# Modulation sums as four quarters, a convolution moved behind a third projection unit, and state-space set-up dealt out evenly, in a two-layer hybrid encoder

## The chip, the cores and the metric

The kernel runs on one core of one Trainium2 chip. What is measured is the device time of one execution in microseconds (us), as the median of several runs. The engines are named as the profile names them: PE is TensorE's matmul side and PEld its weight loads, DVE is VectorE, ACT is ScalarE, POOL is GpSimd, SP is SyncE, whose queue loads the weights. "PEclk" or "granted clock" is TensorE's clock as a share of full speed (1.00 is 2.4 GHz, 0.50 is 1.2 GHz).

## The reference

Two layers, each of them feed-forward, mixer, feed-forward, over 256 positions of width 1024 in float32:

```python
cond = silu(c)[:, None, :]
for l in range(2):
    mod = cond @ mod_w[l] + mod_b[l]               # nine vectors of 1024
    sh1, sc1, g1, sh2, sc2, g2, sh3, sc3, g3 = split(mod, 9)
    h = modulate(rms_norm(x, ffn1_norm[l]), sh1, sc1)
    x = x + 0.5 * g1 * swiglu_ffn(h, w_gu, w_down)      # 1024 -> 2 x 2816 -> 1024
    h = modulate(rms_norm(x, mix_norm[l]), sh2, sc2)
    x = x + g2 * hybrid_mixer(h, ...)    # attention | state space (S5) | convolution
    h = modulate(rms_norm(x, ffn2_norm[l]), sh3, sc3)
    x = x + 0.5 * g3 * swiglu_ffn(h, w_gu, w_down)
return rms_norm(x, final_norm)
```

The state-space part needs, before its layer's mixer, powers of a complex number per state (`PW`), their products with another one (`PQ`), and from these two large tables, W and O, that multiply B and C. The convolution is a depthwise one over 31 positions of 256 channels, after a gate.

## The kernel before

**Weights.** All weights are streamed once, in units of 128x1024, by SP's queue into six buffers `raw`. A matmul in float32 is made of three (`mm3`, L328 to L330): ACT makes the rounded part `hi` of a unit (L100), DVE the rest `lo` (L102, about 1.2 us), and PE takes hi·hi, lo·hi and hi·lo. `hi` and `lo` have six pairs of buffers, five in the mixer. So every unit of weights that PE uses has first passed ACT and then DVE, and PE takes the units in the order of the stream.

**The feed-forward part** goes over 11 blocks of 256 columns of the inner width. For a block, four units make gate and up products in PSUM (`ps_gt`, or `ps_gu` and `ps_gs` at the start), ACT makes silu, DVE the product `h` (L742; L756 at the start) and its `hTl` (L746), and two further units make the down products `ps_y`. The next block's `ps_gt` goes into the bank that `h` frees.

**Modulation.** mod_w of what comes later is streamed between the units of the feed-forward parts. DVE multiplies a half unit by its column of `cond` and adds it to an accumulator `macc` (L365, 128x512, two buffers; eight of them make one half of a vector). When both halves of a vector are there, `mod_flush` sums them over the partitions: a product with a matrix of ones on PE for each half (L389), a copy to `mrow` on ACT (L391), and POOL's DMAs of the row to DRAM and back as columns. Of the 16 flushes, six stand in the first feed-forward part of layer 0 (FFN1 of layer 0), three in its second (FFN2 of layer 0), six in FFN1 of layer 1 and one in FFN2 of layer 1.

**Set-up of the state space.** `ssm_small` and `ssm_layer` are generators that write out a few small instructions and then yield. They are stepped from the feed-forward code: layer 0's by `SSTART` steps for each of eight rounds at the start of the program and then by a hook at every tick of FFN1 of layer 0 (a tick is one unit; 41 ticks), layer 1's at the 45 ticks of FFN2 of layer 0. `SLOTS0` and `SLOTS1` are the first tick, the number of ticks, and the steps. The tables are made of products of 128x512 on DVE (L1011, L1013; sums in L1015), four for each of W and O and for each of two factors.

**The mixer** is written by several threads of code whose turns stand in a list of letters, `MIX_ORDER`: W issues the next unit's products of the input projection (A, C, four of B, four of Q), C is the convolution's thread (`conv_thread`), S the state space's, the others the attention. The convolution's input is written to `uT`, copied by DMAs on ACT's and POOL's queues to `U4` (`U` in the profile) in four shifted copies, and then multiplied in 64 products of 128x256 (L1404, `ps_cv`).

**Order.** The framework's scheduler fixes each engine's order ahead of the run, from the order of the code and modelled times; every engine then takes its list strictly in turn. So an instruction that waits holds up all that stand behind it on its engine.

Of the kernel before, what the change touches and what calls it, by code (L numbers as in the profile page):

```python
# [13 lines left out]
AF = mybir.ActivationFunctionType  # L14
# [12 lines left out]
ADG = (((0,),(1,),(2,3)),((0,1,2,3),))  # L27
HIP = 150
HIPT = 50
SLOTS0 = (4, 40, 2)  # L30
SSTART = 4
SLOTS1 = (2, 60, 2)
UW = 264
NEG_INADM = -3.0e38
NEG_TAKEN = -3.3e38
# [9 lines left out]

MIX_ORDER = """
W K S K K W K J I J J I W I S J S I W I J J I S W I J I J S W C C C I J J I S W
I J I J S I J C S W W C S W a b S N a C a C S S b b a C a b C b a a b b b C b b
b
"""  # L50

# [80 lines left out]
def kernel(  # L132
# [31 lines left out]
    def s2(shape, nm, tg="a", dtype=F32):  # L164
        return two_p.tile(shape, dtype, tag="s2" + tg, name=nm, bufs=S2B[tg])
# [217 lines left out]
    def mod_flush():  # L383
        while len(finished) >= 2:
            l, m, _, acc0 = finished.pop(0)
            acc1 = finished.pop(0)[3]
            ps = bank(ps_m, "ps_mod")
            for h, acc in enumerate((acc0, acc1)):
                nc.tensor.matmul(ps[32 * h:32 * h + 32, :], ones, acc, start=True, stop=True, tile_position=(0, 32 * h))  # L389
            r = s2([64, 512], "mrow")  # L390
            nc.scalar.activation(r, ps[0:64, :], AF.Copy, scale=0.5 if m in (2, 8) else 1.0)  # L391
            d = spill[(l, m)] = tc.dram_tile([1, D], F32, name=f"spill{l}_{m}")
            for h in range(2):
                nc.gpsimd.dma_start(d[:, 512 * h:512 * h + 512], r[32 * h:32 * h + 1, :])  # L394
            if m % 3 != 2:
                nc.gpsimd.dma_start(mc(l, m), d[0].rearrange("(k p) -> p k", p=P))
            if m % 3 == 1:
                nc.gpsimd.tensor_scalar_add(mc(l, m), mc(l, m), 1.0)
                n0 = 8 * (L * (m // 3) + l)
                nc.gpsimd.tensor_mul(mc(l, m), mc(l, m), ncol[:, n0:n0 + 8])  # L400
# [421 lines left out]
    def ssm_small(l):  # L822
# [7 lines left out]
        def B(nm, shape):  # L830
            n = math.prod(shape)
            if not pool8 or pool8[-1][1] + n > 2048:
                pool8.append([b8([P, 2048], "sp_tmp"), 0])
            t_, o_ = pool8[-1]
            pool8[-1][1] += n
            v_ = t_[:, o_:o_ + n]
            return v_ if len(shape) == 1 else v_.rearrange("p (d n) -> p d n", d=shape[0])
# [92 lines left out]
        yield  # L930

        PQr, PQi = B("pqr", [8, NL]), B("pqi", [8, NL])
        u8, v8 = B("u8", [8, NL]), B("v8", [8, NL])
        qrb = qr.rearrange("p (o n) -> p o n", o=1).to_broadcast([P, 8, NL])
        qib = qi.rearrange("p (o n) -> p o n", o=1).to_broadcast([P, 8, NL])
        cmul(PQr, PQi, PWr[:, 0:8, :], PWi[:, 0:8, :], qrb, qib, u8, v8)
        yield

        cA, cB = T("cA", [8, NL]), T("cB", [8, NL])
        lo_, hi_ = slice(0, 64), slice(64, 128)  # L940
        for tau in range(8):
            d_ = 7 - tau
            cp(cA[lo_, tau, :], PQr[lo_, d_, :])
            cp(cA[hi_, tau, :], PQi[hi_, d_, :])
            cp(cB[lo_, tau, :], PQi[lo_, d_, :], -1.0)
            cp(cB[hi_, tau, :], PQr[hi_, d_, :])
            if tau % 2:
                yield
        oA, oB = T("oA", [8, NL]), T("oB", [8, NL])
        cp(oA[lo_], PWr[lo_, 1:9, :])  # L950
        cp(oA[hi_], PWi[hi_, 1:9, :], -1.0)
# [140 lines left out]
    def mixer(l, finish):  # L1092
# [30 lines left out]
        def project():  # L1123

            def xT(k):
                return [v["f"][:, k].rearrange("p t n -> p (t n)") for v in (xTh, xTl)]

            for i in IN_ORDER:
                if i == "A":

                    us = [st.get() for _ in range(4)]
                    pin["A"] = [bank(ps_g, f"ps_in{t}")[:, :328] for t in range(2)]
                    pin["K"] = bank(ps_m, "ps_kT")
                    for t in range(2):
                        for k in range(8):
                            wh, wl = us[k // 2]
                            cs = slice(424 * (k % 2) + 96, 424 * (k % 2) + 424)
                            mm3(pin["A"][t], xTh[t][:, k, :], xTl[t][:, k, :], wh[:, cs], wl[:, cs], k == 0, k == 7)
                    for k in range(8):
                        wh, wl = us[k // 2]  # L1140
                        cs = slice(424 * (k % 2), 424 * (k % 2) + 96)
                        mm3(pin["K"][:96, :256], wh[:, cs], wl[:, cs], *xT(k), k == 0, k == 7)
                        if k % 2:
                            st.done()
                    yield
                elif i == "C":
                    us = [st.get() for _ in range(2)]
                    pin["C"] = bank(ps_g, "ps_inC")
                    for j in range(2):
                        for k in range(8):  # L1150
                            wh, wl = us[k // 4]
                            cs = slice(256 * (k % 4) + P * j, 256 * (k % 4) + P * j + P)
                            mm3(pin["C"][:, 256 * j:256 * j + 256], wh[:, cs], wl[:, cs], *xT(k), k == 0, k == 7)
                            if j and k % 4 == 3:
                                st.done()
                    yield
                else:
                    pin[i] = [bank(ps_g, f"ps_in{i}") for _ in range(2)]
                    for n_ in range(4):
                        wh, wl = st.get()  # L1160
                        o = slice(256 * (n_ // 2), 256 * (n_ // 2) + 256)
                        for k4 in range(4):
                            k = 4 * (n_ % 2) + k4
                            for j in range(2):
                                cs = slice(256 * k4 + P * j, 256 * k4 + P * j + P)
                                mm3(pin[i][j][:, o], wh[:, cs], wl[:, cs], *xT(k), k == 0, k == 7)
                        st.done()
                        yield

# [218 lines left out]
        def conv_thread():  # L1388
# [9 lines left out]
                yield  # L1398
            yield
            pc = abank(1, "ps_cv")  # L1400
            for ct in range(2):
                for b in range(8):
                    for q in range(4):
                        nc.tensor.matmul(pc[32 * q:32 * q + 32, 256 * ct:256 * ct + 256], SS["W4"][:, 32 * ct + 8 * q + b, :],  # L1404
                                         U4[:, q, ct, b:b + 256], start=(b == 0), stop=(b == 7),
                                         tile_position=(0, 32 * q))
# [83 lines left out]
        for g_ in gens:  # L1490
            yield from g_

    def stages(gen, first, n, per):

        def hook(u):
            if first <= u < first + n:
                for _ in range(per):
                    next(gen, None)
            elif u >= first + n:
                for _ in gen:  # L1500
                    pass
        return hook
# [74 lines left out]
```

## Time and profile before

| | |
|---|---|
| time, median of 3 runs | 1168.14 us (1165.55 to 1171.28) |
| time of the profiled execution | 1179.52 us |
| its span | 1177.7 us |
| mean granted clock of TensorE | 0.947 |
| PE, DVE, ACT, POOL busy | 1104.6, 880.2, 574.4, 78.3 us |

The profiled execution took 11.4 us more than the median of the runs. The feed-forward parts lie, in its time, at about 0 to 262 us (the first 70 us are the start: loads, norms and the first blocks), 425 to 620, 640 to 830, and 995 to the end; the mixers between them. An engine's busy time is the time in which at least one of its instructions was under way; instructions on DVE and PE overlap a little, so the distance between the starts of two neighbours is what one costs in a full queue.

### The profile page before, as it was taken

Reading aid. Unit: us, or ns where it says so; the run is one execution under the profiler, and the core shown is the slowest. Engines: PE = TensorE matmul, PEld = TensorE weight load, DVE = VectorE, ACT = ScalarE, POOL = GpSimd, SP = SyncE. Lnnn points to the kernel's source line nnn. Section 1 sums busy time; section 2 is a strip of 40 time slices with the busy share of each in tenths; the row PEclk is TensorE's granted clock in tenths of the full one; section 3 lists DMA queues with packets and bytes.
Section 4 is the critical chain, followed back from the end, with each engine's and each line's share of the span. In section 5 each row is a group of like instructions: output and inputs, shape, how many; then the busy total and the mean of one; then the engine's idle time right before and its main releaser. Section 6 shows DMA issues by size and latency. Waiting matters only on the chain.

```text
span 1177.7 us, 19146 instructions
## 1 busy us (share of the span) xinstructions
PE 1104.6 (94%) x6979; PEld 944.4 (80%) x6979; DVE 880.2 (75%) x1763; ACT 574.4 (49%) x1035; POOL 78.3 (7%) x144
## 2 busy tenths in 40 slices
PE   5959999998989999889998999999899998999996
PEld 3549888877876779788986888888698687999986
DVE  4779888887667888887757888887667677665655
ACT  4484434346427565744445444443553656544442
POOL 5000021000021000001000000100000000000000
PEclk9979989999798999989999999999989699999999
DMA  9957999995452268678773999989355224767651
GB/s 249 295 182 248 310 312 319 325 282 148 122 118 87 90 197 293 207 229 259 226 223 93 331 337 347 321 300 291 101 157 128 90 89 136 246 209 217 212 162 54
DMA packets 181647, 251.44 MB, mean 214 GB/s; under 512 B 18998, under 2 KB 131840, under 8 KB 181552
## 3 DMA queue, kind: packets, MB, share of 16 engines
q1 hardware_dynamic: 173728, 240.56, 63.7%
q0 software_dynamic: 4768, 7.52, 2.9%
q10 hardware_dynamic: 3056, 2.13, 0.8%
q8 instruction: 55, 0.90, 0.3%
q14 instruction: 40, 0.33, 0.1%
HBM read 245.19 MB, written 1.11 MB: 209 GB/s over the span
## 4 chain that ended last, share of the span: by engine, by line
PE 78%; DVE 9%; DMA 7%; ACT 4%; issue 2%; POOL 0%; ACTq 0%; DVEq 0%; SPq 0%; POOLq 0%
PE ps_gt L328 11%; PE ps_gt L330 11%; PE ps_gt L329 11%; PE ps_y L329 7%; PE ps_y L330 7%; PE ps_y L328 7%; DMA raw<-in_mod_w_dram 3%; DVE lo L102 3%; PE ps_mod L389 2%; DMA U<-uT 1%; PE ps_idx L1198 1%; ACT hf L321 1%; PE ps_cv L1404 1%; PE ps_o L1267 1%; PE ps_gu L328 1%
## 5 line engine op out<-in xcount | busy, mean ns | idle before, releaser
L102 DVE TENSOR_TENSOR lo<-raw,hi 128x1024 fp32r<-128x1024 f32 (+1 forms) x314 | 378.6, 1212 | 141.1 <-ACT hi L100 138.4
L100 ACT ACTIVATE hi<-raw 128x1024 fp32r<-128x1024 f32 (+1 forms) x314 | 327.9, 1055 | 298.7 <-PE ps_gt L329 111.8
L328 PE MATMUL ps_gt<-xTh,hi 128*128 128x256 f32 x1120 | 320.6, 288 | 7.1 <-DVE h L742 7.1
L329 PE MATMUL ps_gt<-xTl,hi 128*128 128x256 f32 x1120 | 319.4, 286 | 0.0
L330 PE MATMUL ps_gt<-xTh,lo 128*128 128x256 f32 x1120 | 317.7, 287 | 0.0
L328 PEld LDWEIGHTS ps_gt<-xTh,hi 128*128 128x128 f32 x1120 | 218.0, 195 | 19.3 <-DVE h L742 7.4
L330 PEld LDWEIGHTS ps_gt<-xTh,lo 128*128 128x128 f32 x1120 | 216.9, 195 | 6.7 <-issue 5.9
L329 PEld LDWEIGHTS ps_gt<-xTl,hi 128*128 128x128 f32 x1120 | 218.6, 195 | 1.8 <-issue 0.8
L365 DVE SCALAR_TENSOR_TENSOR macc<-raw,cond,macc 128x512 f32<-128x512 f32 x224 | 166.4, 747 | 26.1 <-DMA raw<-in_mod_w_dram 24.1
L329 PE MATMUL ps_y<-lo,hTh 128*128 128x512 f32 x352 | 139.5, 396 | 0.9 <-DVE lo L102 0.9
L330 PE MATMUL ps_y<-hi,hTl 128*128 128x512 f32 x352 | 138.2, 393 | 1.0 <-DVE hTl L746 1.0
L328 PE MATMUL ps_y<-hi,hTh 128*128 128x512 f32 x352 | 136.9, 394 | 1.3 <-ACT hTh L745 1.2
L329 PEld LDWEIGHTS ps_y<-lo,hTh 128*128 128x128 f32 x352 | 66.8, 190 | 17.3 <-issue 2.5
L330 PEld LDWEIGHTS ps_y<-hi,hTl 128*128 128x128 f32 x352 | 66.8, 190 | 16.1 <-DVE hTl L746 2.1
L328 PEld LDWEIGHTS ps_y<-hi,hTh 128*128 128x128 f32 x352 | 66.6, 189 | 16.1 <-ACT hTh L745 2.6
L394 POOL DMA_DIRECT2D spill<-mrow x32 | 16.1, 508 | 716.1 <-ACT mrow L391 673.1
L740 ACT ACTIVATE silu<-ps_gt 128x256 f32<-128x256 f32 x70 | 25.7, 381 | 57.8 <-PE ps_gt L330 57.6
L742 DVE TENSOR_TENSOR h<-silu,ps_gt 128x256 f32<-128x256 f32 x70 | 28.5, 415 | 23.3 <-ACT silu L740 23.3
L328 PE MATMUL ps_gu<-hi,xTh 128*128 128x512 f32 x96 | 38.5, 402 | 5.9 <-DVE xTh L324 5.9
L330 PE MATMUL ps_gu<-hi,xTl 128*128 128x512 f32 x96 | 38.5, 401 | 3.1 <-DVE xTl L325 3.0
L329 PE MATMUL ps_gu<-lo,xTh 128*128 128x512 f32 x96 | 37.6, 392 | 0.0
L321 ACT ACTIVATE hf<-ps_ada,mcol 128x128 f32<-128x128 f32 x80 | 29.7, 471 | 10.6 <-PE ps_ada L316 8.6
(384 smaller groups left out, 1630.3 us busy)
## 6 DMA issues: line engine op xcount, KB each, us to landing
raw<-in_ffn_w_gu_dram SPq DMA_DIRECT2D x140, 512.0 KB
raw<-in_mod_w_dram SPq DMA_DIRECT2D x128, 512.0 KB
raw<-in_ffn_w_down_dram SPq DMA_DIRECT2D x88, 512.0 KB
raw<-in_ffn_w_gu_dram SPq DMA_DIRECT2D x72, 256.0 KB
raw<-in_w_in_dram SPq DMA_DIRECT2D x20, 512.0 KB
raw<-in_mod_w_dram SPq DMA_DIRECT2D x32, 256.0 KB
raw<-in_w_out_dram SPq DMA_DIRECT2D x16, 512.0 KB
row<-spill POOLq DMA_DIRECT2D x6, 512.0 KB, 3.9
```

Source lines behind the costliest of these rows:

```text
L100: nc.scalar.activation(hi[:, :n], raw[:, :n], AF.Copy)
L102: nc.vector.tensor_sub(lo[:, :n], raw[:, :n], hi[:, :n].bitcast(F32))
L321: hold[t]["hf", h] = nc.scalar.activation(hf[:, k, :], ps[:, P * k:P * k + P], AF.Identity, bias=mc(l, 3 * i)[:, kk:kk + 1], scale=mc(l, 3 ...
L328: return [nc.tensor.matmul(ps, xh, wh, start=start, stop=False), nc.tensor.matmul(ps, xh, wl, start=False, stop=False), nc.tensor.matmul(p ...
L329: nc.tensor.matmul(ps, xh, wl, start=False, stop=False),
L330: nc.tensor.matmul(ps, xl, wh, start=False, stop=stop)]
L365: nc.vector.scalar_tensor_tensor(acc, raw[:, 512 * i:512 * i + 512], cond[:, k:k + 1], prev, op0=ALU.mult, op1=ALU.add)
L389: nc.tensor.matmul(ps[32 * h:32 * h + 32, :], ones, acc, start=True, stop=True, tile_position=(0, 32 * h))
L394: nc.gpsimd.dma_start(d[:, 512 * h:512 * h + 512], r[32 * h:32 * h + 1, :])
L740: nc.scalar.activation(s, ps[i][:, :256], AF.Silu)
L742: nc.vector.tensor_mul(h, s, ps[i][:, 256:])
L1198: nc.tensor.matmul(ps[:, nk * i:nk * i + nk], qiT[32 * b:32 * b + 32, 256 * i + P * t:256 * i + P * t + P], kiT[32 * b:32 * b + 32, :nk], ...
```

## The change

Three edits. First, `mod_flush` makes four products of 128x256 in place of two of 128x512, on the four groups of 32 columns of PE's array, all issued next to each other, with an issue-order mark; the copy to `mrow` is 128x256 in place of 64x512, and four DMAs in place of two write the row. Second, the convolution's products come one turn earlier in `MIX_ORDER` but are held behind the last product of the Q unit that stands there. Third, the set-up: eight rounds of 2 steps at the start in place of 4, then 43 steps dealt evenly over 37 ticks (58 over 42 in layer 1) in place of 2 at each tick; `PQ` is made by doubling (2 copies and 18 products and sums of 128x16 to 128x64 in place of 6 of 128x128), which puts it in the order in which it is used, so that 16 ACT copies of 64x16 for each of `cA` and `cB` (L826) become two of 64x128 each.

```diff
-SLOTS0 = (4, 40, 2)
-SSTART = 4
-SLOTS1 = (2, 60, 2)
+SLOTS0 = (1, 37, 43)
+SSTART = 2
+SLOTS1 = (1, 42, 58)
...
-I J I J S I J C S W W C S W a b S N a C a C S S b b a C a b C b a a b b b C b b
+I J I J S I J S W W C C S W a b S N a C a C S S b b a C a b C b a a b b b C b b
...
-            for h, acc in enumerate((acc0, acc1)):
-                nc.tensor.matmul(ps[32 * h:32 * h + 32, :], ones, acc, start=True, stop=True, tile_position=(0, 32 * h))
-            r = s2([64, 512], "mrow")
-            nc.scalar.activation(r, ps[0:64, :], AF.Copy, scale=0.5 if m in (2, 8) else 1.0)
+            for q in (3, 2, 1, 0):
+                mm_ = nc.tensor.matmul(ps[32 * q:32 * q + 32, 0:256], ones, (acc0, acc1)[q // 2][:, 256 * (q % 2):256 * (q % 2) + 256],
+                                       start=True, stop=True, tile_position=(0, 32 * q))
+                tc.stamp_issue_order_token(mm_.ins, f"mod{l}_{m}")
+            r = s2([P, 512], "mrow")
+            nc.scalar.activation(r[:, 0:256], ps[:, 0:256], AF.Copy, scale=0.5 if m in (2, 8) else 1.0)
...
-            for h in range(2):
-                nc.gpsimd.dma_start(d[:, 512 * h:512 * h + 512], r[32 * h:32 * h + 1, :])
+            for q in range(4):
+                nc.gpsimd.dma_start(d[:, 256 * q:256 * q + 256], r[32 * q:32 * q + 1, 0:256])
...
-        cmul(PQr, PQi, PWr[:, 0:8, :], PWi[:, 0:8, :], qrb, qib, u8, v8)
+        e.tensor_copy(PQr[:, 7, :], qr)
+        e.tensor_copy(PQi[:, 7, :], qi)
+        for n in (1, 2, 4):
+            s_, d_ = slice(8 - n, 8), slice(8 - 2 * n, 8 - n)
+            cmul(PQr[:, d_, :], PQi[:, d_, :], PQr[:, s_, :], PQi[:, s_, :],
+                 PWr[:, n:n + 1, :].to_broadcast([P, n, NL]), PWi[:, n:n + 1, :].to_broadcast([P, n, NL]),
+                 t1[:, :n, :], t2[:, :n, :])
+            yield
...
-        for tau in range(8):
-            d_ = 7 - tau
-            cp(cA[lo_, tau, :], PQr[lo_, d_, :])
-            cp(cA[hi_, tau, :], PQi[hi_, d_, :])
-            cp(cB[lo_, tau, :], PQi[lo_, d_, :], -1.0)
-            cp(cB[hi_, tau, :], PQr[hi_, d_, :])
+        cp(cA[lo_], PQr[lo_])
+        cp(cA[hi_], PQi[hi_])
+        cp(cB[lo_], PQi[lo_], -1.0)
+        cp(cB[hi_], PQr[hi_])
...
-                                mm3(pin[i][j][:, o], wh[:, cs], wl[:, cs], *xT(k), k == 0, k == 7)
+                                hold[i] = mm3(pin[i][j][:, o], wh[:, cs], wl[:, cs], *xT(k), k == 0, k == 7)[-1]
...
             pc = abank(1, "ps_cv")
-            for ct in range(2):
+            with tc.issue_after(hold["Q"].ins):
+              for ct in range(2):
...
-    def stages(gen, first, n, per):
+    def stages(gen, first, n, steps):
...
-                for _ in range(per):
+                i = u - first
+                for _ in range((i + 1) * steps // n - i * steps // n):
                     next(gen, None)
```

DVE's order where the first table W of layer 0 is made, before; `xTl` is the last input of the first blocks, `lo` a unit of weights for PE, `et` a small set-up operation:

```order
L519 TENSOR_TENSOR xTl_118<-hfs_685,xTh_117 128x256
L1011 TENSOR_TENSOR W_757<-bri_704,sp_cA_613 128x512
L1013 TENSOR_TENSOR wtmp_760<-bri_704,sp_cB_614 128x512
L1011 TENSOR_TENSOR W_757<-bri_704,sp_cA_613 128x512
L1013 TENSOR_TENSOR wtmp_764<-bri_704,sp_cB_614 128x512
L1011 TENSOR_TENSOR W_757<-bri_704,sp_cA_613 128x512
L1013 TENSOR_TENSOR wtmp_792<-bri_704,sp_cB_614 128x512
L1011 TENSOR_TENSOR W_757<-bri_704,sp_cA_613 128x512
L1013 TENSOR_TENSOR wtmp_796<-bri_704,sp_cB_614 128x512
L1011 TENSOR_TENSOR sl_O_758<-CRI_721,sp_oA_698 128x512 x4
L1031 TENSOR_TENSOR et_1285<-sl_Ec_1283 128x16
L102 TENSOR_TENSOR lo_768<-raw_601,hi_767 128x1024
```

The same products in the changed kernel, some 60 rows of DVE's list later and among the units of the first whole block of FFN1 of layer 0 (`ps_gt_1152` is that block's bank):

```order
L1014 TENSOR_TENSOR W<-bri,sp_cA 128x512 x4
L365 SCALAR_TENSOR_TENSOR macc<-raw,cond,bias_94 128x512
L1016 TENSOR_TENSOR wtmp<-bri,sp_cB 128x512 x3
L102 TENSOR_TENSOR lo<-raw,hi 128x1024
L1045 TENSOR_TENSOR CmDd<-dKm,ident 128x256
L1014 TENSOR_TENSOR sl_O<-CRI,sp_oA 128x512 x4
L1034 TENSOR_TENSOR et<-sl_Ec 128x16
L1035 TENSOR_TENSOR et<-sl_Es 128x16
L365 SCALAR_TENSOR_TENSOR macc<-raw,cond,macc 128x512
L1018 TENSOR_TENSOR W<-W,wtmp 128x512 x3
L102 TENSOR_TENSOR lo<-raw,hi 128x1024
L745 TENSOR_TENSOR h<-silu,ps_gt_1152 128x256
```

Twelve products with no `lo` among them have become seven, a `lo`, four, three sums and a `lo`; they still stand ahead of an `h`. In FFN2 of layer 0, DVE's order has three `lo` between the first product of W and the `h` of the block under way; in the changed kernel it has four there, since the products come earlier in the stream of units. Up to the end of FFN1 of layer 0, 50 set-up instructions that were made before the first row of the upper fence now come behind it (37 of 128x16, 6 of 128x32, 6 of 128x64, one of 128x256).

PE's order around the convolution's products in layer 0, before (`ps_inQ` are the Q units of the projection):

```order
L329 MATMUL ps_inQ<-xTl,hi 128x256
L330 MATMUL ps_inQ<-xTh,lo 128x256
L1404 MATMUL ps_cv<-U_3393,sl_W_1674 32x256 x64
L328 MATMUL ps_inQ<-xTh,hi 128x256
L329 MATMUL ps_inQ<-xTl,hi 128x256
```

and in the changed kernel, where `ps_yT` (state space) follows:

```order
L329 MATMUL ps_inQ<-xTl,hi 128x256
L330 MATMUL ps_inQ<-xTh,lo 128x256
L1408 MATMUL ps_cv<-U_3403,sl_W_2488 32x256 x64
L1356 MATMUL ps_yT<-ident,ye 128x4x32 x4
L328 MATMUL ps_inQ<-xTh,hi 128x256
```

Before, 34 Q products stood ahead of the convolution since the last other work and 38 between it and `ps_yT`; now all 72 stand ahead of it. It is the same in layer 1.

On PE's list the two halves of the first modulation sum stood 70 rows apart, and the four quarters are neighbours. Thirteen of the 16 flushes had halves apart, three had them next to each other (two in FFN2 of layer 0, the one of FFN2 of layer 1); now all are one piece.

## Rows read from the trace of the kernel before

**Rows 1.** The page: PE's busy time, and the chain that ended last.

```profile
PE 1104.6 (94%) x6979; PEld 944.4 (80%) x6979; DVE 880.2 (75%) x1763; ACT 574.4 (49%) x1035; POOL 78.3 (7%) x144
...
PE 78%; DVE 9%; DMA 7%; ACT 4%; issue 2%; POOL 0%; ACTq 0%; DVEq 0%; SPq 0%; POOLq 0%
```

**Rows 2.** Windows: FFN1 layer 0, FFN2 layer 0, a part, FFN1 layer 1.

```profile
70.40:262.30 191.90, 179.82 (x1117) 154.56 (x1116) 167.89 (x256) 83.90 (x125) 17.40 (x30) 0.94 0.88 287
425.00:615.00 190.00, 182.87 (x1212) 167.08 (x1211) 149.90 (x285) 95.23 (x164) 12.17 (x22) 0.96 0.77 245
495.00:515.00 20.00, 12.87 (x80) 12.38 (x79) 20.00 (x36) 4.73 (x7) 0.00 (x0) 0.74 0.65 204
645.00:825.00 180.00, 180.00 (x1167) 156.77 (x1166) 149.96 (x195) 77.38 (x105) 12.12 (x19) 1.00 0.96 319
```

Columns: window, its length, then busy time of PE, PEld, DVE, ACT and POOL (instructions), granted clock, DMA share, GB/s.

**Rows 3.** Waits of PE in the whole span: us, times, longest.

```profile
PE ps_gt L328 <- DVE h L742: 7.1, 1, 7.1
PE ps_hT L765 <- DVE h L756: 6.2, 1, 6.2
...
PE ps_cv L1404 <- DMA U<-uT: 5.3, 3, 3.6
...
PE ps_gs L329 <- DVE lo L102: 4.2, 1, 4.2
...
PE ps_gs L328 <- ACT hi L100: 1.0, 1, 1.0
```

**Rows 4.** PE's timeline around one half of a sum: start, duration.

```profile
119.59 0.39 PE L330 MATMUL ps_y<-hi,hTl 128*128 128x512 f32 x1
119.91 1.04 PE L389 MATMUL ps_mod<-macc,ones 128*32 128x512 f32 x2
120.89 0.39 PE L328 MATMUL ps_gt<-xTh,hi 128*128 128x256 f32 x1
```

**Rows 5.** The same around two halves that stand next to each other.

```profile
602.34 0.39 PE L330 MATMUL ps_y<-hi,hTl 128*128 128x512 f32 x1
602.66 1.05 PE L389 MATMUL ps_mod<-macc,ones 128*32 128x512 f32 x4
603.64 0.39 PE L328 MATMUL ps_gt<-xTh,hi 128*128 128x256 f32 x1
603.87 0.28 PE L329 MATMUL ps_gt<-xTl,hi 128*128 128x256 f32 x1
603.99 0.29 PE L330 MATMUL ps_gt<-xTh,lo 128*128 128x256 f32 x1
```

**Rows 6.** Line L389: how long PE waited for the accumulator, in all.

```profile
  DVE macc L365: 0.2, 1
```

**Rows 7.** PE's timeline, the convolution's first products in layer 0.

```profile
335.83 1.49 PE L1404 MATMUL ps_cv<-U,sl_W 128*32 128x256 f32 x12 [3.56 <-DMA U<-uT]
```

**Rows 8.** Windows in which the granted clock is low, columns as in rows 2.

```profile
80.00:90.00 10.00, 3.81 (x14) 2.84 (x13) 10.00 (x15) 3.84 (x7) 0.00 (x0) 0.50 0.84 274
90.00:100.00 10.00, 10.00 (x73) 10.00 (x73) 9.49 (x21) 3.62 (x7) 0.00 (x0) 0.82 0.60 189
...
500.00:510.00 10.00, 6.13 (x28) 6.13 (x29) 10.00 (x17) 1.89 (x5) 0.00 (x0) 0.50 0.48 144
```

**Rows 9.** DVE's timeline, table W of layer 0 and the next `lo`.

```profile
70.36 0.68 DVE L1011 TENSOR_TENSOR W<-bri,sp_cA 128x512 f32<-128x512 f32 x1
...
77.69 1.21 DVE L102 TENSOR_TENSOR lo<-raw,hi 128x1024 fp32r<-128x1024 f32 x1
```

**Rows 10.** DVE's timeline in FFN2 of layer 0: small set-up, W, `h`.

```profile
481.37 0.17 DVE L888 TENSOR_TENSOR sp_tmp<-sp_er 128x16 f32<-128x16 f32 x1
481.46 0.17 DVE L889 TENSOR_TENSOR sp_tmp<-sp_ei 128x16 f32<-128x16 f32 x1
...
487.75 0.69 DVE L1011 TENSOR_TENSOR W<-bri,sp_cA 128x512 f32<-128x512 f32 x1 [1.82 <-ACT sp_cA L826]
...
503.40 0.41 DVE L742 TENSOR_TENSOR h<-silu,ps_gt 128x256 f32<-128x256 f32 x1
```

More of the change, by code (lines that the diff above doesn't have):

```diff
@@ L932, in ssm_small @@
         PQr, PQi = B("pqr", [8, NL]), B("pqi", [8, NL])
-        u8, v8 = B("u8", [8, NL]), B("v8", [8, NL])
-        qrb = qr.rearrange("p (o n) -> p o n", o=1).to_broadcast([P, 8, NL])
-        qib = qi.rearrange("p (o n) -> p o n", o=1).to_broadcast([P, 8, NL])
-        cmul(PQr, PQi, PWr[:, 0:8, :], PWi[:, 0:8, :], qrb, qib, u8, v8)
-        yield
+        e.tensor_copy(PQr[:, 7, :], qr)
[6 more added lines that the diff above has]
+            yield
         cA, cB = T("cA", [8, NL]), T("cB", [8, NL])
         lo_, hi_ = slice(0, 64), slice(64, 128)
-        for tau in range(8):
-            d_ = 7 - tau
-            cp(cA[lo_, tau, :], PQr[lo_, d_, :])
-            cp(cA[hi_, tau, :], PQi[hi_, d_, :])
-            cp(cB[lo_, tau, :], PQi[lo_, d_, :], -1.0)
-            cp(cB[hi_, tau, :], PQr[hi_, d_, :])
-            if tau % 2:
-                yield
+        cp(cA[lo_], PQr[lo_])
+        cp(cA[hi_], PQi[hi_])
+        cp(cB[lo_], PQi[lo_], -1.0)
+        cp(cB[hi_], PQr[hi_])
+        yield
         oA, oB = T("oA", [8, NL]), T("oB", [8, NL])
```

## The prediction

> **What bounds the kernel.** I read the page's first part and the chain first. PE is busy for 94% of the span, and 78% of the chain that ended last is PE's [rows 1]. So time is won where PE works less, waits less or runs at full clock, and a saving elsewhere counts only where PE waits for that engine. The windows then say it by stage: in FFN1 of layer 1 PE is busy for 180.00 of 180.00 us at full clock; in FFN1 of layer 0 for 179.82 of 191.90 at 0.94; in FFN2 of layer 0 for 182.87 of 190, and there 20 us hold only 12.87 at clock 0.74 while DVE is busy for all 20.00 [rows 2]. The list of PE's waits names what ends them: 4.2 and 6.2 us in the start of FFN1 of layer 0, 7.1 us in FFN2 of layer 0, all three for DVE, and 5.3 us at the convolution for a DMA [rows 3]. The first two stand behind table W: DVE starts it at 70.36 and comes to the next `lo` only at 77.69 [rows 9]. In FFN2 of layer 0, W begins at 487.75 and the `h` that PE waits for runs at 503.40 [rows 10].
>
> **Modulation sums.** Alone, a half takes 1.04 us on the timeline; by starts, 119.59 to 120.89 is 1.30 us, of which 0.23 belongs to the `ps_y` product ahead of it (the pace of 128x512), so it costs 1.07 [rows 4]. Two halves next to each other cost 602.34 to 603.64, 1.30 as well [rows 5]: two column groups run beside each other, and the second is free. So before, 13 split flushes at 2.14 and three at 1.07 cost 31.0 us. A flush of four quarters should cost what one quarter costs. The trace has none of that size. The pace of the other products is 0.23 us for 128x512 and 0.12 for 128x256 [rows 4, 5], which would make a quarter 0.53, the lower bound; 1.07 is the upper one, if the size doesn't matter. I take 0.65, near the lower one because of that pace, with an estimated 0.12, one product more, for the start that doesn't halve. With 0.65, 16 flushes cost 10.4, and 20.6 us go: 8.9 in each FFN1 (six split flushes), 1.49 + 2 x 0.42 = 2.3 in FFN2 of layer 0, 0.4 in the last part. With 1.07 it is 13.9.
>
> The Trainium skill (TensorEngine Tiling (Array Packing), Key Properties) says that tiles work independently but that a change of tiling mode drains TensorE. The trace agrees on the first [rows 5]; of the second no run here shows how much of the 1.07 us it is. By that rule a split flush pays the drain twice and a joint one once, so the gain of the 13 would hold even if a quarter's own cost didn't halve.
>
> In FFN1 of layer 1 PE is the bound [rows 2], so the 8.9 count there; I take 8, because the units must arrive faster and DMA is at 0.96 already [rows 2]. FFN2 of layer 0 and the last part give 2.7. FFN1 of layer 0 follows below. ACT's copy and POOL's two more DMAs for each flush are off the path: POOL is busy for 7% [rows 1]. If that cover were gone it would be as much as POOL's and the DMA's landing time before the last columns, which are needed at the next norm.
>
> **Convolution.** PE waits 3.56 us in layer 0 and then runs the products [rows 7]; of the 5.3 us in three waits [rows 3] 1.7 are left for layer 1. Now 38 more Q products stand ahead, at a start-to-start of 0.12 us 4.6 us of work, more than any of the waits, so all 5.3 should go; the lower end is 1.7, if the DMAs land later by as much as PE comes later. What stands behind the convolution comes 1 us later at most; ACT takes it up as soon as PE ends it, and 24 Q products still lie between it and its transposes. If Q's weights were not ready, the wait for them would take its place; nothing in rows 3 shows PE waiting for a Q unit.
>
> **PQ, cA and cB.** Each layer loses 32 ACT copies for four longer ones. In layer 0 they stand ahead of the `hi` for which PE waits 1.0 us in the start [rows 3]. I count that and an estimated 0.5 for the clock behind it, 1.5 us, from 0 to 3. DVE gets 2 copies and 18 operations in place of 6; small ones are 0.09 us apart [rows 10].
>
> **Set-up in FFN1 of layer 0.** PE's two waits are 10.4 us. Around them the clock is 0.50 with 3.81 busy and then 0.82 of 10 us [rows 8], 1.9 + 1.8 = 3.7 us lost. With the sums' 8.9 PE could win 10.4 + 3.7 + 8.9 = 23 of 191.9. But DVE was busy for 167.89 of these [rows 2], and it gets 50 more set-up instructions (front section): at 0.09 to 0.18 us, 5 to 9. So DVE needs 173 to 177. It can't be full all the time, since each `lo` waits for its `hi`. At a share of 0.97 that is 178 to 182, at the 0.875 of now 198 to 202, at 1.00 173. I take 182: in the 20 us where PE waits for DVE it is full [rows 2], and only stretches where PE holds DVE back lower the share. That makes 10 us, with ends at -10 and 19. What is late next is not PE's work but DVE's, the bound of this stage from now on.
>
> **Set-up in FFN2 of layer 0.** The 7.1 us and half the 6.13 at clock 0.50 [rows 8], 3.1, are there to win. The products of W still stand in a piece ahead of an `h`, with four `lo` among them where three were. The piece was 503.40 - 487.75 = 15.65 us [rows 10]; with one more `lo` and its sum of some 1.2 + 0.7 us it is about 17.5. A unit of weights is 24 products of 0.12 us, 2.8 us of PE's time, and the two down units are 5.5. PE has four units of a block, then the down units, before it needs `h`; with the piece starting one to two units earlier for PE than before, a wait of 1 to 3 us is left. I take 7 of the 10.2, with ends at 0 and 10. DVE has room over the stage: 149.9 of 190 [rows 2].
>
> **Sum.** Start 1.5, FFN1 of layer 0 10, convolution 5.3, FFN2 of layer 0 2.3 + 7, FFN1 of layer 1 8, last part 0.4: 34.5 us, in a profiled execution of 1179.5 us, which is 11.4 above the median. The terms are waits and work that are there in either, so I take them from the median: 1168.1 - 34.5 = 1133.6, say 1133.
>
> **Rivals.** (A) The forecast, 1133, own range 1124 to 1143. (B) DVE takes most of it: FFN1 of layer 0 ends no earlier than now with a share of 0.90 (192 to 197, -3), and the wait in FFN2 stays. Left are 1.5 + 5.3 + 2.3 + 8 + 0.4 - 3 = 14.5, or 1154. For it: the two pieces are still there in DVE's order, and DVE is the bound; against: the seven and four products now have a `lo` between them. (C) Everything comes: DVE full in FFN1 of layer 0 (19), all of FFN2 of layer 0 (12.5), 8.9 in FFN1 of layer 1, 5.3, 3 and 0.4: 49, or 1119. For it: DVE is full whenever PE waits for it; against: no stage of 190 us shows it over 0.88 [rows 2]. (D) Slower: the accumulators. Both halves are now read at once, by an instruction that PE takes in turn, from two buffers. If the second half is late, PE waits with all its matmuls behind it; and DVE can't begin the next vector until PE has read both. At w us for each of the 12 flushes in the two FFN1, the gain is gone at 34.5 / 12 = 2.9 us, and w = 4 gives 1168.1 - 34.5 + 48 = 1182. For it: DVE becomes the bound of FFN1 of layer 0, so its sums come late; against: before, PE waited 0.2 us in all for an accumulator [rows 6]. (E) No change: the groups don't overlap at this size, and a flush costs 2.14 as two halves apart did; then B's 14.5 lose the 10.7 of the sums and the three joint flushes 3.2 more, which leaves 0.6, or 1167. Two halves that cost as much as one [rows 4, 5] speak against it.
>
> **Chances.** A 0.53, B 0.17, C 0.17, D 0.06, E 0.07. Within 0.5% (5.8 us), about what a measurement of this kernel can tell from no change, lies E alone; slower is D; faster are A, B and C with 0.87. The range reaches from 1115, below C, to 1156, above B, and leaves out D, E and the outer tails.
>
> **What would show it.** A group of four quarters of about 0.65 us between its neighbours' starts, none over 1.1. No wait of `ps_cv` for U. In FFN1 of layer 0 DVE's share at 0.95 or more, the stage near 180 us, and PE's waits there small and spread; no `h` or `lo` wait over 3 us, in FFN2 of layer 0 neither. FFN1 of layer 1 8 us shorter and PE still full. The prediction is wrong if DVE's share in FFN1 of layer 0 stays at 0.88 with PE waiting, if PE waits for `macc` by more than a few us in all, or if DMA holds FFN1 of layer 1.

## The result, and the profile after

The changed kernel takes 1156.8 us (median of 15 runs, 1150.2 to 1167.1) against 1171.3 us of the kernel before in 15 runs (1164.9 to 1179.9): a ratio of 0.9874, 95% interval 0.9847 to 0.9901. It is 14.5 us faster, where 34.5 were forecast; 1156.8 lies just above the range, which ended at 1156. A ratio, here and below, leaves out executions that took over 1.5% more than the fastest one of the same kernel. The changed kernel's profiled execution took 1159.4 us, 20 less than the one of before, which was 8 us above its kernel's median.

The page of the changed kernel, busy time and chain [rows 1]:

```profile
PE 1082.1 (93%) x7043; PEld 936.8 (81%) x7043; DVE 881.8 (76%) x1791; ACT 557.9 (48%) x979; POOL 93.2 (8%) x176
...
PE 56%; DMA 7%; DVE 6%; ACT 3%; issue 2%; SPq 1%; ACTq 0%; DVEq 0%
```

PE's work fell by 22.5 us, about what the sums should save (20.6), but its idle time did not fall: it is 75.4 us of the span, after 73.1. The shares of this chain add up to 75% of the span only, for it goes back no further than 284 us; so its 56% for PE can't be set beside the 78% of before, and FFN1 of layer 0 isn't in it. Where the time went is told by the starts of the first `ps_ada` (L316) of each norm, which cut the span into stages; the first of them is at 271.3 us before and at 272.3 in the changed kernel:

| us | start and FFN1 layer 0 | mixer 0 | FFN2 layer 0 | FFN1 layer 1 | mixer 1 | FFN2 layer 1 |
|---|---|---|---|---|---|---|
| before | 271.3 | 137.7 | 218.7 | 209.3 | 137.7 | 203.0 |
| changed | 272.3 | 141.0 | 212.1 | 202.0 | 127.4 | 202.6 |
| difference | +1.0 | +3.3 | -6.6 | -7.3 | -10.3 | -0.4 |
| forecast | -11.5 | -3.6 | -9.3 | -8.0 | -1.7 | -0.4 |

FFN1 of layer 1 and the last part are as forecast. FFN1 of layer 0 is off by 12.5 us. Three of the windows of rows 2 (columns: PE, PEld, DVE, ACT, POOL, clock, DMA share, GB/s), then three of 10 us:

```profile
70.40:262.30 191.90, 174.68 (x1146) 153.61 (x1145) 170.96 (x305) 83.16 (x132) 19.85 (x38) 0.96 0.87 281
425.00:615.00 190.00, 184.37 (x1253) 169.33 (x1253) 155.97 (x310) 96.16 (x150) 15.90 (x28) 0.98 0.77 246
645.00:825.00 180.00, 179.46 (x1227) 162.61 (x1226) 154.71 (x205) 79.36 (x112) 17.30 (x31) 1.00 0.97 325
...
80.00:90.00 10.00, 9.56 (x81) 9.56 (x82) 9.12 (x29) 5.96 (x14) 0.00 (x0) 1.00 0.80 280
...
120.00:130.00 10.00, 8.34 (x48) 7.04 (x48) 10.00 (x19) 5.19 (x15) 2.51 (x5) 1.00 0.48 159
...
150.00:160.00 10.00, 7.55 (x62) 6.60 (x62) 8.48 (x17) 2.39 (x3) 2.87 (x5) 1.00 0.73 232
```

The old hole is gone: 80 to 90 us has PE busy for 9.56 at full clock, where it was 3.81 at half [rows 8]. New ones stand from 120 us on, and the loads slow down there too, with DMA shares of 0.48 and 0.73. DVE's share of the stage is 0.89, not the 0.95 or more of the forecast. PE's waits, whole span [rows 3]:

```profile
PE ps_gt L328 <- DVE h L745: 6.6, 3, 3.9
...
PE ps_y L328 <- ACT hi L100: 4.5, 2, 2.7
PE ps_gt L330 <- DVE lo L102: 4.4, 6, 1.8
```

No `ps_cv` stands among them. What stands there now are three waits for `h`, the longest of 3.9 us in FFN2 of layer 0, and many short ones for `hi` and `lo`. `hi` itself waits for data. In 110 to 250 us, waits of ACT and of SP's queue, before (first fence) and changed (second); L426 and L429 are the loads of gate and up weights:

```profile
ACT hi L100 <- DMA raw<-in_ffn_w_gu_dram: 32.3, 17, 4.5
...
SPq L426 <- DVE macc L365: 5.3, 7, 1.0
```

```profile
ACT hi L100 <- DMA raw<-in_ffn_w_gu_dram: 57.2, 23, 5.1
...
SPq L429 <- DVE macc L365: 11.1, 11, 3.2
```

This is the chain that these lines suggest: a gate or up load waits for a buffer that an accumulation still holds (5.3 us before, 11.1 after), so the weights land late, so ACT and then PE wait. Over all loads of these 140 us, though, SP's waits for accumulations are some 41 us in both kernels. More than one edit lies between the two; kernels that differ by one come below. Counted over the 48 modulation loads of this stage, a buffer was held from the issue of its load to the end of its last accumulation for 10.9 us in the mean before and 13.1 after (sum of ends less sum of issue times, by 48).

The sums themselves, around one flush of four quarters [rows 4, 5]:

```profile
482.35 0.39 PE L330 MATMUL ps_y<-hi,hTl 128*128 128x512 f32 x1
482.67 0.64 PE L390 MATMUL ps_mod<-macc,ones 128*32 128x256 f32 x8
483.24 0.39 PE L328 MATMUL ps_gt<-xTh,hi 128*128 128x256 f32 x1
```

From start to start 0.89, less 0.23: 0.66 us a flush; 0.65 was forecast.

### The profile page after: what moved, and what is told of

Same layout as the page of the kernel before. It is cut to its first block, busy times and chain, and to the rows that moved or that the text cites. A ratio compares the mean times of both kernels' runs of the same rounds, so it can differ in the third digit from the quotient of the medians.

```text
span 1157.5 us, 19306 instructions
## 1 busy us (share of the span) xinstructions
PE 1082.1 (93%) x7043; PEld 936.8 (81%) x7043; DVE 881.8 (76%) x1791; ACT 557.9 (48%) x979; POOL 93.2 (8%) x176
## 4 chain that ended last, share of the span: by engine, by line
PE 56%; DMA 7%; DVE 6%; ACT 3%; issue 2%; SPq 1%; ACTq 0%; DVEq 0%
PE ps_gt L328 7%; PE ps_gt L329 7%; PE ps_gt L330 7%; PE ps_y L330 5%; PE ps_y L328 5%; PE ps_y L329 5%; DMA raw<-in_mod_w_dram 3%; DMA raw<-in_ffn_w_gu_dram 2%; DVE lo L102 2%; DVE macc L365 2%; ACT hi L100 1%; PE ps_idx L1201 1%; PE ps_gu L328 1%; PE ps_gu L330 1%; PE ps_cv L1408 1%
## 5 line engine op out<-in xcount | busy, mean ns | idle before, releaser
L328 PE MATMUL ps_gt<-xTh,hi 128*128 128x256 f32 x1120 | 320.2, 288 | 10.4 <-DVE h L745 6.6
L330 PEld LDWEIGHTS ps_gt<-xTh,lo 128*128 128x128 f32 x1120 | 214.4, 193 | 6.2 <-DVE lo L102 5.7
L328 PE MATMUL ps_y<-hi,hTh 128*128 128x512 f32 x352 | 133.6, 396 | 4.9 <-ACT hi L100 4.5
L397 POOL DMA_DIRECT2D spill<-mrow x64 | 31.3, 496 | 642.0 <-ACT mrow L394 640.5
L745 DVE TENSOR_TENSOR h<-silu,ps_gt 128x256 f32<-128x256 f32 x70 | 28.0, 417 | 10.6 <-ACT silu L743 10.4
L748 ACT ACTIVATE hTh<-h 128x256 fp32r<-128x256 f32 x70 | 27.4, 410 | 16.6 <-DVE h L745 15.5
```

Of the source, the lines that this page charges most:

```text
L328: return [nc.tensor.matmul(ps, xh, wh, start=start, stop=False), nc.tensor.matmul(ps, xh, wl, start=False, stop=False), nc.tensor.matmul(p ...
L330: nc.tensor.matmul(ps, xl, wh, start=False, stop=stop)]
L397: nc.gpsimd.dma_start(d[:, 256 * q:256 * q + 256], r[32 * q:32 * q + 1, 0:256])
L745: nc.vector.tensor_mul(h, s, ps[i][:, 256:])
L748: nc.scalar.activation(hi, h, AF.Copy)
```

## The experiments

The times of all of them, with the ratio to the kernel before in runs on the same chip, and from their profiles the start with FFN1 of layer 0, FFN2 of layer 0, FFN1 of layer 1, and the mean hold of a modulation buffer in FFN1 of layer 0:

| | time | ratio, 95% | FFN1 l0 | FFN2 l0 | FFN1 l1 | hold |
|---|---|---|---|---|---|---|
| quarters alone | 1170.6 | 0.9993 (0.9958 to 1.0029) | 275.1 | 212.7 | 204.1 | 13.0 |
| set-up alone | 1163.7 | 0.9923 (0.9883 to 0.9964) | 259.9 | 211.0 | 212.7 | 11.8 |
| convolution alone | 1173.3 | 1.0015 (0.9984 to 1.0045) | 267.6 | 219.2 | 209.1 | 10.8 |
| set-up queued step by step | 1159.5 | 0.9891 (0.9852 to 0.9929) | 275.8 | 205.9 | 201.4 | 13.9 |
| without quarters | 1159.8 | 0.9910 (0.9877 to 0.9944) | 263.0 | 213.0 | 211.3 | 11.8 |
| quarters in pairs | 1156.7 | 0.9899 (0.9851 to 0.9947) | 265.6 | 209.6 | 206.3 | 12.4 |
| three accumulators | 1158.6 | 0.9909 (0.9875 to 0.9943) | 264.6 | 211.5 | 203.5 | 12.1 |
| mixed | 1149.1 | 0.9804 (0.9750 to 0.9857) | 260.8 | 209.5 | 199.8 | 11.9 |
| joint halves | 1158.3 | 0.9878 (0.9839 to 0.9917) | 273.4 | 212.4 | 203.0 | 13.6 |
| quarters alone, three accumulators | 1160.2 | 0.9916 (0.9887 to 0.9945) | 262.4 | 215.5 | 201.5 | 10.7 |
| mixed, queued step by step | 1157.3 | 0.9887 (0.9831 to 0.9944) | 271.2 | 209.5 | 202.1 | 12.6 |
| mixed, layer 1 queued step by step | 1147.8 | 0.9813 (0.9778 to 0.9848) | 266.1 | 209.1 | 200.2 | 11.9 |
| without the convolution's move | 1157.6 | 0.9897 (0.9847 to 0.9946) | 271.1 | 212.5 | 202.1 | 13.3 |
| mixed, without the convolution's move | 1154.2 | 0.9857 (0.9801 to 0.9912) | 260.7 | 212.7 | 201.9 | 11.9 |

Mixed is the kernel with halves in the six flushes of FFN1 of layer 0 and quarters in the other ten. A stage of one profile is good to some 4 to 5 us: the convolution alone and the kernel before run the same code in FFN1 of layer 0 and took 267.6 and 271.3, and two of the mixed ones 260.8 and 266.1.

**Each part alone.** The first thought, theory P, was that the products of W and O, which still stand in rows in DVE's list (front section), cost again what they had cost at 80 us.

The kernel before with the quarters alone:

```diff
-            for h, acc in enumerate((acc0, acc1)):
+            for q in (3, 2, 1, 0):
...
```

> The kernel before with the four quarters alone; the set-up, its tables and the convolution stay where they were. A flush should cost 0.66 us on PE as it does in the changed kernel, so 20.4 us of PE's work go, 8.9 of them in each of the two FFN1. Theory P (the pieces: in the changed kernel the products of tables W and O stand in a row in the middle of DVE's list, hold up the lo and the accumulators behind them, so that buffers come free late and the loads stop): here the pieces are still at the start, FFN1 of layer 0 is PE's from 95 us on, and gets shorter by 6 to 9 us; in all about 1152. Theory T (in all: FFN1 of layer 0 is held by DVE's and DMA's whole work, and PE's saving is worth nothing there): FFN1 of layer 0 within 2 us of before, in all about 1161.

The time did not move, where the theories had 1152 and 1161, and FFN1 of layer 0 got no shorter (275.1), against P's 6 to 9 us. In FFN1 of layer 1 the same edit gave 5.2 us. So the saving is lost with the quarters alone, without the new set-up.

The set-up and PQ alone:

```diff
-SLOTS0 = (4, 40, 2)
-SSTART = 4
-SLOTS1 = (2, 60, 2)
+SLOTS0 = (1, 37, 43)
+SSTART = 2
+SLOTS1 = (1, 42, 58)
...
```

> The kernel before with the set-up's slots and the new PQ, cA and cB alone; the sums stay two halves, the convolution stays. Theory P: the waits at 79 and 88 us go (10 us) but the pieces come back around 115 to 170 us, with loads stopped behind them (DMA share under 0.8 over some tens of us) and PE waiting for hi and lo afterwards; FFN1 of layer 0 from -2 to +6 us against before, FFN2 of layer 0 5 shorter, in all 1165 to 1172. Theory T: FFN1 of layer 0 is DVE's, gets 3 to 5 us longer from the start of the program because DVE has 5 us more, and the waits of PE are spread with no stop of the loads; in all about 1168. The two differ in the DMA share by 10 us windows, not in the time.

1163.7, and FFN1 of layer 0 11.4 us shorter, below what either theory said.

The convolution alone:

```diff
-I J I J S I J C S W W C S W a b
+I J I J S I J S W W C C S W a b
...
+            with tc.issue_after(hold["Q"].ins):
...
```

> The kernel before with the convolution's products behind the third Q unit alone. All theories: PE's waits for U (5.3 us in three) are gone in both layers and nothing takes their place, so about 1166, 5 less than before, somewhat more if the clock in layer 0 stays full there. A rival: the transposes behind the convolution wait for ACT instead, then less than 2 us are won.

No wait of `ps_cv` is left in its profile, and the time did not fall, where 5 us less was expected: 1.0015, with an interval that leaves 1.9 us of gain at most.

The changed kernel with each set-up step queued behind the `lo` of its tick:

```diff
-                for _ in range((i + 1) * steps // n - i * steps // n):
-                    next(gen, None)
+                with tc.issue_after(st.last_lo.ins):
+                    for _ in range((i + 1) * steps // n - i * steps // n):
+                        next(gen, None)
...
```

> The changed kernel, and each step of the set-up is queued on DVE behind the lo that was prepared last at its tick, so that the products of W and O can't stand in a row. The same work on every engine. Theory P: no window with the DMA share under 0.8 between 110 and 250 us, PE waits there for 3 us at most in all, FFN1 of layer 0 ends 8 to 14 us earlier than in the changed kernel, in FFN2 of layer 0 the wait of 3.9 us for h goes; in all 1140 to 1147. Theory T: the same DVE work in the same stage, so within 3 us of the changed kernel, 1154 to 1158.

The rows of products are gone from DVE's list (at most three stand together now), and FFN1 of layer 0 takes 275.8. FFN2 of layer 0 took 205.9, 6 us less than in the changed kernel, as P says for that stage; two later runs with this edit don't repeat it (below). For FFN1 of layer 0, P has fallen; T, which says that this stage can't get shorter, fell with the set-up alone. The next theory, H, came from the hold: the joint flush reads the accumulators of both halves at once. Before, each half's accumulator was read when it was ready, and freed for the next vector. With two of them in all, the next vector now can't begin until the flush.

**Who holds the buffers.** The changed kernel with the old sums:

```diff
-            for q in (3, 2, 1, 0):
+            for h, acc in enumerate((acc0, acc1)):
...
```

> The changed kernel with the sums as they were, two halves. The runs so far: FFN1 of layer 0 (start to the first product of the mixer's norm) took 271.3 us before, 259.9 with the set-up alone, 275.1 with the quarters alone and 272.3 with both; a load buffer of modulation was held from the issue of its load to its last use for 10.9, 11.8, 13.0 and 13.1 us. Theory H (held buffers: the joint flush reads both halves' accumulators at once, there are only two, so the next vector's accumulation starts late, its load buffers are held longer, and the six buffers stand in the way of the weights): here the hold is under 12 us, FFN1 of layer 0 takes 258 to 263 us, FFN1 of layer 1 about 210 in place of 202; in all 1150 to 1155. Theory N (the 259.9 was one lucky execution): 268 to 273 there, and 1160 to 1166 in all.

The stage is as H says, 263.0 with a hold of 11.8, and FFN1 of layer 1 is back at 211. In 110 to 250 us SP's waits for accumulations are some 32 us over all loads, where the changed kernel, with the same set-up, has 41; of the gate and up loads they are

```profile
SPq L426 <- DVE macc L365: 4.7, 10, 1.5
```

in place of 11.1. The whole, 1159.8, is 5 us above H's range and at the edge of N's; N's 268 to 273 for the stage did not come.

Each half summed by itself, as two quarters:

```diff
-            for q in (3, 2, 1, 0):
+            for q in (1, 0, 3, 2):
...
-                tc.stamp_issue_order_token(mm_.ins, f"mod{l}_{m}")
+                tc.stamp_issue_order_token(mm_.ins, f"mod{l}_{m}_{q // 2}")
```

> The changed kernel, but each half is summed by itself, as two quarters on two column groups next to each other, as soon as its accumulator is there. A flush then costs PE two times 0.66 = 1.3 us, 0.7 more than the four quarters; POOL's four DMAs and the copy stay as changed. Theory H: the hold falls to under 12 us, FFN1 of layer 0 takes 260 to 265 us, FFN1 of layer 1 203 to 207; in all 1146 to 1153. Theory M (the quarters cost by something else than the joint reading: by the size, by the four DMAs of POOL, by their place on PE): FFN1 of layer 0 stays over 270, in all 1156 to 1162.

265.6 and a hold of 12.4, both just outside what H says: most of the loss is undone, with the quarters' size and POOL's four DMAs unchanged. The whole does not show it: 1156.7 is M's, and the changed kernel's.

Three accumulators:

```diff
-                        s["acc"] = two_p.tile([P, 512], F32, tag="macc", name="macc", bufs=2)
+                        s["acc"] = two_p.tile([P, 512], F32, tag="macc", name="macc", bufs=3)
```

> The changed kernel with three accumulators in place of two; all the work is the same. Theory H: the next vector's first half can start before the joint flush, the hold falls to under 12 us, FFN1 of layer 0 takes 258 to 264 us, FFN1 of layer 1 stays near 202; in all 1143 to 1149. Theory M: within 3 us of the changed kernel, FFN1 of layer 0 over 270.

264.6 and 12.1, close to what H says for the stage. The whole does not show it: 1158.6 in eleven runs is as M says. In the profiled execution, which is the median one, the two mixers took 274.5 us, 6.1 more than in the changed kernel's profile, which takes most of the stage's 7.7 us back; why, is not shown. What the third accumulator does is seen at a flush, in the changed kernel (first fence) and with three accumulators (second); the operand `bias` marks the first accumulation of a half:

```profile
150.17 0.64 PE L390 MATMUL ps_mod<-macc,ones 128*32 128x256 f32 x8
152.84 0.75 DVE L365 SCALAR_TENSOR_TENSOR macc<-raw,cond,bias 128x512 f32<-128x512 f32 x1
```

```profile
141.76 0.75 DVE L365 SCALAR_TENSOR_TENSOR macc<-raw,cond,bias 128x512 f32<-128x512 f32 x1
...
150.12 0.64 PE L390 MATMUL ps_mod<-macc,ones 128*32 128x256 f32 x8
```

In the changed kernel the next vector starts only after the flush has started, 0.6 to 3.1 us later, here and at the other four flushes of this stage that a vector follows. With three accumulators it starts 2 to 11 us ahead of the flush, at all five. That is H's mechanism in the trace.

Halves in the six flushes of FFN1 of layer 0, quarters in the other ten:

```diff
+            nfl[0] += 1
+            if nfl[0] <= 6:
+                for h, acc in enumerate((acc0, acc1)):
+                    nc.tensor.matmul(ps[32 * h:32 * h + 32, :], ones, acc, start=True, stop=True, tile_position=(0, 32 * h))
...
+            else:
```

> The changed kernel, the first six flushes (those of FFN1 of layer 0) as two halves as before, the other ten as four quarters. Theory H: FFN1 of layer 0 as without quarters, 258 to 263 us, FFN1 of layer 1 202; in all 1143 to 1149. Theory N: FFN1 of layer 0 268 to 273, in all 1155 to 1160.

As H says: 260.8, and 1149.1, the upper end of its range and faster than both kernels. Its profiled execution was its fastest run (1137.9), so its stages are on the low side.

Two halves of 128x512, read next to each other:

```diff
-            for q in (3, 2, 1, 0):
+            for h in (1, 0):
...
```

> The changed kernel with two halves of 128x512 in place of four quarters, still read next to each other when both accumulators are there; the copy and the two DMAs as before the change. Each flush costs PE 1.07 us in place of 0.66. Theory H (it is the joint reading that holds the load buffers): hold about 13 us, FFN1 of layer 0 272 to 277 us, FFN1 of layer 1 204 to 207; in all 1158 to 1165. Theory M (it is the quarters' size, or POOL's four DMAs): hold under 12 us, FFN1 of layer 0 260 to 266, in all 1150 to 1155.

273.4, with a hold of 13.6: the size of the products is not the cause, reading them together is. Of its waits in 110 to 250 us (L428 loads gate and up weights here):

```profile
SPq L428 <- DVE macc L365: 11.6, 10, 5.0
```

The weight loads wait for accumulations as in the changed kernel, with another size of product; over all loads it is 45.5 us.

The kernel before with the quarters and three accumulators, the edits of the first and the seventh run:

> The kernel before with the four quarters and three accumulators; set-up and convolution as before. With two accumulators FFN1 of layer 0 took 275.1 us and the whole 1170.6. Theory H: the hold goes from 13.0 to about 12, FFN1 of layer 0 takes 264 to 268, less than the kernel before, and the quarters' saving shows: in all 1157 to 1163. Theory M: 275 and 1168 to 1172.

262.4 in place of 275.1, and 1160.2 in place of 1170.6, by a third accumulator alone. The window of 110 to 250 us, in this kernel and then in the one with the quarters alone:

```profile
110.00:250.00 140.00, 137.81 (x974) 125.64 (x973) 126.78 (x185) 57.85 (x85) 20.54 (x37) 0.99 0.98 326
```

```profile
110.00:250.00 140.00, 131.52 (x905) 118.37 (x903) 113.98 (x166) 50.62 (x74) 16.85 (x34) 0.98 0.90 294
```

The loads run at 326 GB/s in place of 294, and PE is busy for 6 us more of the 140. ACT still waits 52.3 us for gate and up weights, as much as with the joint halves (52.4), so ACT's wait by itself is not what costs the time. In this kernel the 10.5 us of waits at the old hole are still there, and yet the stage takes what the set-up alone gave (259.9). With the set-up and the third accumulator both (264.6) it is no shorter. The two gains don't add.

**What is left of P.** Mixed, with each set-up step queued behind a `lo`, by the edit of the fourth run:

> Halves in the first six flushes and quarters in the others, and each set-up step queued on DVE behind the lo prepared last at its tick, in both layers. Is there anything in the pieces once the accumulators are out of the way? Theory P: the stop of the loads of 8.6 us near 111 us goes and FFN1 of layer 0 takes 253 to 258 in place of 260.8; the wait for h in FFN2 of layer 0 goes, 204 to 207 in place of 209.5; in all 1137 to 1143. Without P: FFN1 of layer 0 259 to 264, FFN2 of layer 0 205 to 210, in all 1145 to 1152.

271.2, 10 us longer than without the queueing, and 1157.3: slower. FFN2 of layer 0 took 209.5, as without it. Queueing each step behind a `lo` is worse in FFN1 of layer 0 than rows of products; whether by the fine pieces or by the tie to a `lo`, these runs don't tell.

The same in layer 1's set-up alone, against the run before it:

```diff
-                with tc.issue_after(st.last_lo.ins):
+                with tc.issue_after(st.last_lo.ins) if steps == SLOTS1[2] else ExitStack():
```

> As the last, but only layer 1's set-up (in FFN2 of layer 0) is queued behind the lo; layer 0's is as in the changed kernel. FFN1 of layer 0 259 to 263 by every theory; FFN2 of layer 0 204 to 207, with no wait for h over 2 us, by P, 209 to 212 without; in all 1142 to 1147 by P, 1147 to 1151 without.

1147.8 and 209.1 in FFN2 of layer 0: no gain over mixed, by either measure. FFN1 of layer 0, with the code of the mixed kernel, took 266.1, where every theory had 259 to 263.

**Is the convolution's step in the time?** The changed kernel, and the mixed one, with the edit of the third run taken back:

> The changed kernel with the convolution's products where they stood before the change. In the profiles so far the two mixers together took 270 to 278 us with the old place (four profiles) and 263 to 275 with the new one (ten), 6.5 us less in the mean; in the timed runs of the new place alone no gain showed. If the place is worth its 5.3 us of waits: mixers 270 to 278, in all 1159 to 1165, against 1157 with it. If the clock or another wait gives it back: mixers as with it, in all 1154 to 1159.

> The kernel with halves in the first six flushes and quarters after, with the convolution's products at the old place. The same with the new place took 1149.1. If the place is worth its waits: 1152 to 1157, mixers 270 to 278; if not: 1146 to 1151.

PE's waits for U are there again (3.5 and 4.3 us), and the two mixers took 268.4 and 269.5 us. The first time, 1157.6, is as expected of a place that is worth nothing, the second, 1154.2, as of one that is worth its waits. The pairs of kernels that differ by this step alone, by their ratios: 0.9874 and 0.9897, 0.9804 and 0.9857, 0.9910 and 0.9923, 1.0015 and 1. In the mean that is 0.2% or 2 us, each with an uncertainty of 0.3 to 0.8%. The profiles say more: over all sixteen, the two mixers took 267.4 us in the mean with the new place (ten, 262.6 to 274.5) and 272.3 with the old one (six, 268.4 to 278.0). The waits go; that their 5.3 us come is not shown, and in the five other profiles with the old place they were 2.9 to 4.3.

## Why the prediction was wrong

**The step that failed** is the sum of FFN1 of layer 0: "That makes 10 us", with the start 11.5, where the stage became 1.0 us longer. Its two parts stand apart now. With the new set-up and split halves the stage took 259.9, 263.0, 260.8, 266.1 and 260.7, a mean of 262.1, against 271.3 and 267.6 of the old one: 7 us shorter. With the joint flush of two accumulators and the same set-up it took 272.3, 273.4 and 271.1, 10 us more (and 275.8 where the steps were queued as well). The prediction counted the quarters' 8.9 us there as a gain that only DVE's share would cap, and put the joint reading of the accumulators at nothing; together they were a loss of 10, and that is the miss. By the stages of the two profiles it makes 12.5 of the 20 us that are missing; FFN2 of layer 0 makes 2.7 and FFN1 of layer 1 0.7.

The whole time bears this out in part. Split halves in this stage alone took the ratio from 0.9874 to 0.9804, and, within the noise, from 0.9897 to 0.9857 without the convolution's move; the third accumulator took it from 0.9993 to 0.9916 with the old set-up. With the new set-up neither the third accumulator (0.9909) nor the pairs (0.9899) made the kernel faster, though the stage was 7 to 8 us shorter in their profiles.

**The rival that named the mechanism** was D: "DVE can't begin the next vector until PE has read both". It was priced as PE waiting for an accumulator, with rows 6 against it, and given 0.06. PE never waited so: no accumulator stands in the list of what it waited for at line L390. DVE did wait for PE there, a little:

```profile
  DVE macc L365: 3.7, 4
```

The price came by another way, through the six load buffers: the next vector begins behind the flush (the fences above), so accumulations come later and hold their buffers longer, 13.1 us in place of 11.8 with the same set-up; the weight loads behind wait, and the wait shows as `hi` for DMA. That the joint reading with two accumulators costs the time is shown by the runs; that it does so by the buffers is read from these waits. Against it stands the kernel with the set-up queued, as long in this stage (275.8), whose gate and up loads wait for accumulations for 1.1 us only. The price is 10 us over six flushes, 1.7 each. In FFN1 of layer 1 the joint flush cost nothing that can be seen (202.0 with two accumulators, 203.5 and 201.5 with three), so the forecast's 8 came (7.3). Only the stream stands on DVE there; that this is the reason was not tested.

**What bounds FFN1 of layer 0** was put down to DVE alone, at a share of 0.97. DVE's share was 0.89 with PE waiting, close to what the prediction had named as a sign that it is wrong, and DMA's was 0.87. The floor of about 260 us is there, though: set-up alone, quarters with three accumulators, and both, end at 260 to 265, with DVE at 0.90 to 0.92. What sets it is not settled; DVE, DMA and PE are each busy for about nine tenths and are tied by six buffers.

**Right:** the quarter (0.66 us), FFN1 of layer 1 and the last part; the 10.4 us of waits at 79 and 88 us, of which 1.5 are left, and the clock behind them. **Half right:** FFN2 of layer 0 gave 6.6 of 9.3; the 7.1 us wait is 1.0, and a new one of 3.9 stands one block later, again for `h` behind DVE (19.97 of the 20 us from 512 on busy). Alone, the quarters and the set-up each gave about as much there (212.7 and 211.0 against 218.7), so these two gains don't add either. **Not shown:** the convolution's 5.3 us. **Near by luck:** the rival B's sum, 1154. Its FFN1 of layer 0 came as it said, no shorter and with DVE at 0.89 for its 0.90, but not for its reason, the work on DVE: with the same set-up and split halves the stage was 7 us shorter. And B kept the wait in FFN2.

## What to carry to other kernels

Before two reductions are joined to save work on one engine, ask what the operands of the first one hold meanwhile: here the joint sum kept an accumulator, this a load buffer, and this the weights of the engine that was to be relieved. A stall that stands in no list of waits by its own name can be found from the loads' queue: look what its issues wait for, and how long a buffer is held, in kernels that differ by one edit. And an edit is right or wrong by the stage: the same quarters gained 7 us in one feed-forward part and lost 10 in another; the kernel that keeps them out of FFN1 of layer 0 is 2.0% faster than before (1.4 to 2.5%), with the rest of the change.

## What the runs showed of the hardware

The time of this kernel moves with the granted clock from one execution to the next. Over the 15 runs of the changed kernel its mean was 0.957, 0.961 and 0.960 in the three fastest (1150.2 to 1152.1 us) and 0.943 in the slowest (1167.1). Within the profiled execution, products of the attention stood at 0.50 in one mixer, with PE busy all the time, and at 0.93 in the other (141.0 and 127.4 us):

```profile
372.30:382.30 10.00, 10.00 (x41) 8.21 (x41) 4.77 (x15) 4.79 (x15) 0.00 (x0) 0.50 0.03 2
...
917.50:927.50 10.00, 9.79 (x63) 8.06 (x64) 6.78 (x26) 8.30 (x28) 0.55 (x1) 0.93 0.14 52
```

So the -10.3 us of the second mixer in the table of stages can't be put down to the change, and a gain of 5 us in a mixer can't be read from one profile. Four column groups of 128x256 cost PE 0.66 us together, two of them 0.64 (the quarters in pairs, from start to start less 0.23), and two of 128x512 1.07 [rows 5]: what counts is the size of one group, not how many there are. The Trainium skill (TensorEngine Tiling (Array Packing), Key Properties) says that different tiles can execute in parallel; the trace agrees, with 1.07 us for two groups of 128x512 as for one [rows 4, 5].
